# Two mixers issued in the order of the text: ScalarE and VectorE under a hand-written order, with the norm's column moved into the first segment

## The chip, the cores and the metric

The kernel runs on one core of one Trainium2 chip. The metric is the device time of one execution in microseconds; the median over several runs is what two kernels are compared by. The core has five engines that matter here, each with a queue of its own: TensorE (PE in the profile; its weight loads are shown apart, as PEld), VectorE (DVE), ScalarE (ACT), GpSimd (POOL) and SyncE (SP, which issues the loads). An engine issues its instructions in the order in which they stand in its queue, and an instruction waits on semaphores until what it needs is there.

## The reference

A decoder trunk of two layers on one sequence of 256 tokens, 1024 wide, 16 heads of 64, in float32. Each layer is: half a SwiGLU block, a mixer, half a SwiGLU block.

```python
h = x
for layer in range(2):
    h = h + 0.5 * swiglu(rmsnorm(h, ffn1_norm[layer]), gate1, up1, down1)
    hn = rmsnorm(h, mix_norm[layer])
    if layer == 0:
        h = h + mixer_a(hn, ...)     # causal attention, three dilated windows merged
    else:
        h = h + mixer_b(hn, ...)     # causal attention on shared keys and values
    h = h + 0.5 * swiglu(rmsnorm(h, ffn2_norm[layer]), gate2, up2, down2)
    if layer == 0:
        shared = shared_kv(h, kv_norm, kv_w)   # keys and values of layer 1
return rmsnorm(h, final_norm)
```

With 256 tokens the three windows of mixer A become one attention with a mask that holds the logarithm of how often each key counts, and mixer B is plain causal attention. `swiglu(h)` is `(silu(h @ gate) * (h @ up)) @ down`, 2816 wide inside. `rmsnorm` divides each token by the root of its mean square and multiplies by a gain.

## The kernel before

**Numbers in two parts.** Every product is made from high and low parts: a weight piece is loaded raw, ScalarE copies it to the high part (`wh_...`), VectorE subtracts to get the low part (`wl_...`), and TensorE runs high*high, high*low and low*high. So each weight piece costs one ScalarE copy of 128x1024 and one VectorE subtraction of 128x1024 ahead of its products, and activations are treated alike (`parts_of`: a ScalarE copy, and `rest`, a VectorE subtraction). The pieces lie in a ring of eight buffers for `wh` and eight for `wl`; a ninth split waits until TensorE has finished the products of a piece whose buffer comes free.

**The stream** lies transposed in `hT` (part of the tensor `gains_hT`), eight blocks of 128 features by 256 tokens. For each norm, `scale(k)` makes `x_n_k`, block k times its gain in two parts, and `square(k)` makes the square on ScalarE (`sq_n_k`) and adds it into `ss_n` on GpSimd: seven adds, one behind the other, as all go into one tile. `finish()` then multiplies `ss_n` with a column of 1/1024 on TensorE (`col_n`), adds epsilon on VectorE (`v_n`) and raises to -0.5 on GpSimd (`c_n`): the factor of each token. The factor is applied after the products. In the FFN `spread()` also turns it into a row (`diag_n`, `row_n`, `r_n`).

**The mixers.** `mixer` first runs six segments of projections (`projections`), then the output projection (`out_t`). A segment is 16 products: eight blocks of features for two tiles of 128 tokens, in the order features 0 to 3 for tile 0, then tile 1, features 4 to 7 for tile 0, then tile 1. `evacuate` scales a finished tile out of PSUM with the norm's factor; VectorE rotates queries and keys (`rotate`); `turn_in` transposes them on TensorE (`qt`) and splits them (`qkh`, `qkl`); then for each of eight pairs of heads come `scores` (`s`, `sm`, softened by ScalarE, scaled by GpSimd), `turn` (`pt`, split into `pT`) and `values` (`po`, then `o` and `oT`, the blocks of the output projection). In mixer A the first segment needs the norm's factor as soon as it is finished; in mixer B the first segment belongs to another norm, whose factor is known, and the second needs the new one. `out_t` multiplies the eight `oT` blocks with the pieces of `wo` (`wh_ao`, `wl_ao`; `bo` in B) into four accumulators; the last three blocks are held back, and the accumulators finish one after the other; each is added to `hT`, and `scale(d)` follows, and after all eight the eight `square(d)`.

**What sets the order.** The mixers' text is written by an `Agenda`: every step of attention is put on it with a delay, counted in the estimated time of the products, and comes up when the products written so far have passed that time. That gives the order of the text. Behind it, a scheduler goes over the whole program, estimates durations, and lets each engine issue whatever it thinks ready first; the order in an engine's queue is the scheduler's, not the text's. `Pieces` splits weight pieces `LEAD = 4` ahead of their use. The FFN behind a mixer takes its weights by `unit` (`wh_f_g_0`, `wh_f_g_4`, `wh_f_u_0`, `wh_f_u_4`: the two halves of gate and up for two blocks of the inner width). The first such pair of blocks (inner blocks 0 and 1) is multiplied feature by feature, as the `x_n_k` arrive (lines 389 to 404), and then `finish()` writes the column; the pairs 2, 4 and so on follow whole.

Of the kernel before, what the change touches and what calls it, by code (L numbers as in the profile page):

```python
# [29 lines left out]
LEAD = 4  # L30
# [36 lines left out]
def trunk(ctx: ExitStack, tc: tile.TileContext, a: dict, out: bass.AP):  # L67
# [70 lines left out]
    def late_constants():  # L138
        nc.sync.dma_start(rot, a["rot"].rearrange("t p c n -> p t c n"))
        nc.sync.dma_start(masks, a["masks"].rearrange("i p n -> p i n"))  # L140
        nc.sync.dma_start(gfin, a["final_norm"].rearrange("(o d) -> o d", o=1).to_broadcast([P, D]))


    def unit(name, k, n, srcs):

        raw = rawp.tile([P, k, n], F32, tag="raw", name=f"raw_{name}")
        for dst, src in srcs:
            nc.sync.dma_start(raw if dst is None else raw[:, :, dst], src)
        return pieces_of(name, raw, k, n)

    def pieces_of(name, raw, k, n):
        pieces = []
        for j in range(0, k, 1024 // n):
# [4 lines left out]
            nc.scalar.activation(wh, r, AF.Copy)  # L158
            nc.vector.tensor_sub(wl, r, wh.bitcast(F32))  # L159
# [18 lines left out]
    def rows(w, k0, k, c0, n):  # L178
        return w[k0 * P:(k0 + k) * P, c0:c0 + n].rearrange("(k p) n -> p k n", p=P)
# [104 lines left out]
    class Pieces:  # L284
# [29 lines left out]
                    self.rest.pop(0)()  # L314

        def __getitem__(self, i):
            self.split(i + LEAD)
            return self.parts[i]


# [16 lines left out]
        parts_of(hi, lo, flat(q), later=rest.append)  # L337
        return rest

    def ffn_blocks(name, wg, wu, norm, first=None, beside=(), sums=None):  # L340

# [41 lines left out]
        for f in range(0, KF, 2):  # L383
            if f == 0 and first is not None:
                ws = opening(wg, wu, first)
            else:
                ws = zip(*[unit(f"{name}_{n}{f}", KD, S, [(None, rows(w, 0, KD, f * P, S))])
                           for n, w in (("g", wg), ("u", wu))])
            if f == 0:
                acs = [[(trt if i and n == "u" else acc)(f"{name}_{n}{i}") for n in "gu"] for i in range(2)]  # L390
                for k, pair in enumerate(ws):
                    for i in range(2):
                        for ac, (wh, wl) in zip(acs[i], pair):
                            cols = slice(i * P, (i + 1) * P)
                            products_t([ac], [[(wh[:, cols], wl[:, cols])]], norm.x[k:k + 1], k == 0, k == KD - 1)
                    while norm.late:
                        norm.late.pop(0)()
                if first is not None:
                    for k in range(KD - 2, KD):
                        norm.square(k)  # L400
                if norm.col is None:
                    norm.finish()
                done += [(i, *acs[i]) for i in range(2)]
                continue
            pair = list(zip(*ws))
            for call in beside[f // 2 - 1:f // 2]:
                call()
            for i in (f, f + 1):
                acs = both(i, pair)
                close_all()  # L410
                done.append((i, *acs))
# [14 lines left out]
                                for j in range(2))  # L426
        return sums

    def ffn(name, layer, which, norm, after, first=None, beside=(), homes=("kx4", "kx6", "qkh", "qkh")):
        wg, wu, wd = (a[f"ffn{which}_w_{n}"][layer] for n in ("gate", "up", "down"))  # L430
        sums = left_sums(homes)
        blocks = ffn_blocks(name, wg, wu, norm, first, beside, sums)
        if which == 1:
            table(AF.Exp, blocks[-1][:, 0, 0:1].bitcast(F32))
        down(f"{name}_d", wd, blocks, sums, after)
# [141 lines left out]
                part(t, slice(512 + S, 1024), True)  # L577
            after(t)

    def out_t(name, pieces, base, blocks, norm, tail=3):  # L580

        accs = [acc(f"ot_{name}_{i}") for i in range(KD // 2)]

# [8 lines left out]
                nc.tensor.matmul(ac, wl[:, d], hi, start=False, stop=k == KD - 1 and j == 1)  # L592

        for k in range(KD - tail):
            ws = pieces[base + k][0]
            while len(blocks) <= k:
                yield None
            for i in range(KD // 2):
                step(i, k, ws)
                yield 0.72  # L600
# [26 lines left out]
    def attention(agenda, operands, mask, name, blocks):  # L627
# [38 lines left out]
        def turn(p, i):  # L666
            tr = trt(f"pt_{name}{p}_{i}")[:, :3 * P]
            for n in range(3):
                nc.tensor.transpose(tr[:, n * P:(n + 1) * P], sms[p, i][:, n * P:(n + 1) * P], ident)
            pT = pTs[p, i] = pp.tile([P, 2, 3 * P], F32R, tag="pT", name=f"pT_{name}{p}_{i}")  # L670
            parts_of(pT[:, 0], pT[:, 1], tr, later=agenda.soon)

        def values(p):
            g, b = divmod(p, HG // 2)
# [26 lines left out]

        return scores, turn, values

    def mixer(name, segs, plan, wo, mask, after):

# [17 lines left out]
        for norm in {id(norm): norm for norm, _, _ in segs}.values():  # L723
            for i in range(len(norm.late)):
                agenda.after(1.5 + 0.5 * i, lambda norm=norm: norm.late.pop(0)())
        scores, turn, values = attention(agenda, lambda g: (qks[g], vss.get(g)), mask, name, blocks)

        def turns(p):
# [18 lines left out]
        def evacuate(i, t, r, ac, parts):  # L747
# [40 lines left out]

    def first(k, n):
# [21 lines left out]
    def ending(at):  # L811
# [28 lines left out]
    blocks = ffn_blocks("f21", a["ffn2_w_gate"][1], a["ffn2_w_up"][1], n6, beside=[lambda: None] + turns, sums=sums)  # L840

    parts = [[], []]
    outs = [[None, None] for t in range(NT)]
# [63 lines left out]
```

## Time and profile before

| | |
|---|---|
| median of 3 runs | 984.71 us (984.63 to 985.41) |
| the profiled execution | 984.39 us, of which 982.6 us from the first to the last instruction |
| TensorE busy | 968.3 us, 99% of the span |
| VectorE, ScalarE, GpSimd busy | 813.0, 613.8, 289.6 us |
| granted TensorE clock | 0.999 |
| first product of mixer A, first product of the FFN behind it | 190.45 us, 310.02 us |
| first product of mixer B, first product of the FFN behind it | 674.84 us, 793.62 us |

Times are microseconds from the start of the span unless marked ns. A row of the timeline has the start, the duration, the engine, the line, the operation, what it writes and reads (buffer numbers left out), how many instructions are merged into the row, and in brackets how long the engine was idle before it and what released it. Rows of one engine overlap by a little, since an instruction starts while the one before drains. The ends of matmuls are modelled, so their starts are read: from one start to the next.

### The profile page before, as it was taken

The numbers are of one execution on the slowest core, as the hardware profiler recorded it, in microseconds if no ns is written. First come the engines' busy times: TensorE is split into PE (matmuls) and PEld (weight loads), VectorE is DVE, ScalarE is ACT, GpSimd is POOL, SyncE is SP. The second block draws the span as 40 slices with busy tenths as digits, with TensorE's granted clock in tenths as the row PEclk, the third lists the DMA queues.
The fourth block names the chain that finished last, engine by engine and source line by source line (L and its number), as shares of the span: only waits on it lengthen the run. The fifth ranks groups of instructions, "written<-read, shape, count | busy, mean of one in ns | idle before, by whom it ended". The sixth has DMA issues, their size and how long they took to land.

```text
span 982.6 us, 14865 instructions
## 1 busy us (share of the span) xinstructions
PE 968.3 (99%) x5391; PEld 832.8 (85%) x5391; DVE 813.0 (83%) x1383; ACT 613.8 (62%) x1131; POOL 289.6 (29%) x242
## 2 busy tenths in 40 slices
PE   8999999999999999999999999999999999999997
PEld 6888888878889888888888888888788998888886
DVE  7988899887878788889898888987678778888995
ACT  7656657567776566556576655656577766666561
POOL 3211246132342211146032121612142422112461
PEclk9999999999999999999999999999999999999999
DMA  9876636664443565545755555483744345565351
GB/s 317 256 238 186 197 132 217 223 203 155 132 129 106 179 201 178 185 158 210 256 168 176 172 182 205 171 283 109 248 131 129 101 158 170 177 204 180 129 171 43
DMA packets 126857, 176.00 MB, mean 179 GB/s; under 512 B 3392, under 2 KB 106304, under 8 KB 126784
## 3 DMA queue, kind: packets, MB, share of 16 engines
q1 hardware_dynamic: 125936, 174.01, 54.4%
q10 hardware_dynamic: 848, 1.05, 0.3%
q8 instruction: 42, 0.69, 0.3%
q14 instruction: 31, 0.25, 0.1%
HBM read 173.99 MB, written 1.05 MB: 178 GB/s over the span
## 4 chain that ended last, share of the span: by engine, by line
PE 68%; ACT 2%; DVE 2%; issue 1%; POOL 0%; POOLq 0%; ACTq 0%; DVEq 0%
PE f_g L195 12%; PE f_u L195 12%; PE f_u L198 6%; PE f_g L198 6%; PE dn_f_d L188 5%; PE dn_f_d L186 5%; PE dn_f_d L184 5%; PE dn_f_d_m L188 1%; PE dn_f_d_m L186 1%; PE dn_f_d_m L184 1%; PE q_b L184 1%; PE q_b L188 1%; PE q_b L186 1%; PE ot_ao L592 1%; PE ot_ao L590 1%; PE kv_b L184 1%
## 5 line engine op out<-in xcount | busy, mean ns | idle before, releaser
L357 POOL TENSOR_TENSOR j_f_u<-j_f_u,r_n 128x256 f32<-128x256 f32 x88 | 92.3, 1051 | 360.9 <-DVE j_f_u L325 338.1
L195 PE MATMUL f_g<-x_n,wh_f_g 128*128 128x512 f32 x688 | 180.5, 394 | 0.0
L195 PE MATMUL f_u<-x_n,wh_f_u 128*128 128x512 f32 x688 | 177.2, 390 | 0.0
L195 PEld LDWEIGHTS f_u<-x_n,wh_f_u 128*128 128x128 f32 x688 | 129.2, 188 | 27.3
L195 PEld LDWEIGHTS f_g<-x_n,wh_f_g 128*128 128x128 f32 x688 | 124.0, 189 | 22.7
L159 DVE TENSOR_TENSOR wl_f_u<-raw_f_u,wh_f_u 128x1024 fp32r<-128x1024 f32 x86 | 113.1, 1317 | 2.7 <-ACT wh_f_u L158 2.7
L159 DVE TENSOR_TENSOR wl_f_g<-raw_f_g,wh_f_g 128x1024 fp32r<-128x1024 f32 x86 | 104.1, 1229 | 3.9 <-ACT wh_f_g L158 3.9
L198 PE MATMUL f_u<-x_n,wl_f_u 128*128 128x256 f32 x688 | 103.3, 283 | 0.0
L198 PE MATMUL f_g<-x_n,wl_f_g 128*128 128x256 f32 x688 | 102.7, 282 | 0.0
L198 PEld LDWEIGHTS f_g<-x_n,wl_f_g 128*128 128x128 f32 x688 | 96.4, 190 | 6.3
L158 ACT ACTIVATE wh_f_u<-raw_f_u 128x1024 fp32r<-128x1024 f32 x86 | 87.9, 1048 | 13.4 <-PE f_g L195 7.5
L158 ACT ACTIVATE wh_f_g<-raw_f_g 128x1024 fp32r<-128x1024 f32 x86 | 89.5, 1048 | 5.0 <-PE f_g L195 2.8
L198 PEld LDWEIGHTS f_u<-x_n,wl_f_u 128*128 128x128 f32 x688 | 91.6, 192 | 0.0
L355 ACT ACTIVATE j_f_g<-j_f_g 128x256 f32<-128x256 f32 x88 | 36.7, 417 | 87.2 <-DVE j_f_g L354 86.9
L233 POOL TENSOR_TENSOR ss_n<-ss_n,sq_n 128x256 f32<-128x256 f32 x42 | 38.4, 914 | 148.3 <-ACT sq_n L232 146.3
L98 ACT ACTIVATE act_f<-j_f_g 128x256 fp32r<-128x256 f32 x58 | 23.9, 418 | 56.6 <-DVE j_f_g L365 56.6
L365 DVE TENSOR_TENSOR j_f_g<-j_f_g,j_f_u 128x256 f32<-128x256 f32 x58 | 27.9, 487 | 30.1 <-POOL j_f_u L357 30.1
L473 POOL TENSOR_TENSOR sum_f_d_6b<-sum_f_d_6ac,raw_f_d 128x512 f32<-128x512 f32 x4 | 45.5, 11374 | 17.6 <-DVE sum_f_d_6ac L472 13.2
L325 DVE TENSOR_TENSOR j_f_g<-f_g,j_f_g 128x256 f32<-128x256 f32 x88 | 36.7, 417 | 11.9 <-ACT j_f_g L324 11.9
L664 POOL TENSOR_SCALAR sm_b<-sm_b,ls_b 128x128 f32<-128x128 f32 (+1 forms) x32 | 29.8, 949 | 44.0 <-DVE ls_b L662 34.3
L664 POOL TENSOR_SCALAR sm_a<-sm_a,ls_a 128x128 f32<-128x128 f32 (+1 forms) x32 | 28.0, 890 | 50.0 <-DVE ls_a L662 32.8
L324 ACT ACTIVATE j_f_u<-f_u 128x256 f32<-128x256 f32 x88 | 33.0, 375 | 14.7 <-PE row_n L250 13.7
(565 smaller groups left out, 2386.5 us busy)
## 6 DMA issues: line engine op xcount, KB each, us to landing
raw_f_d<-in_ffn_w_down_dram SPq DMA_DIRECT2D x44, 1024.0 KB, 5.0
raw_f_g<-in_ffn_w_gate_dram SPq DMA_DIRECT2D x43, 1024.0 KB, 5.4
raw_f_u<-in_ffn_w_up_dram SPq DMA_DIRECT2D x43, 1024.0 KB, 5.4
raw_qka<-in_a_w_qkv_dram SPq DMA_DIRECT2D x16, 512.0 KB, 4.9
raw_va<-in_a_w_qkv_dram SPq DMA_DIRECT2D x4, 1024.0 KB, 6.0
raw_ao<-in_a_w_o_dram SPq DMA_DIRECT2D x4, 1024.0 KB, 4.9
raw_kvb<-in_kv_w_dram SPq DMA_DIRECT2D x8, 512.0 KB, 4.4
raw_qb<-in_b_w_q_dram SPq DMA_DIRECT2D x4, 1024.0 KB, 5.5
```

Source lines behind the costliest of these rows:

```text
L158: nc.scalar.activation(wh, r, AF.Copy)
L159: nc.vector.tensor_sub(wl, r, wh.bitcast(F32))
L184: nc.tensor.matmul(ac, xh, wh, start=first, stop=False)
L186: nc.tensor.matmul(ac, xh, wl, start=False, stop=False)
L188: nc.tensor.matmul(ac, xl, wh, start=False, stop=last)
L195: nc.tensor.matmul(ac, wh, flat(x), start=first and i == 0, stop=False)
L198: nc.tensor.matmul(ac[:, :S], wl, x[:, 0, :], start=False, stop=last and i == len(ws) - 1)
L233: nc.gpsimd.tensor_tensor(self.ss, self.ss, sq, op=ALU.add)
L325: nc.vector.tensor_add(s, ac[:, :S], s)
L357: nc.gpsimd.tensor_tensor(u, u, norm.row, op=ALU.mult)
L473: nc.gpsimd.tensor_tensor(b[:, 0], ac[:, 0], raw[:, 3], op=ALU.add)
L664: nc.gpsimd.tensor_scalar(sm[:, seg], sm[:, seg], ls[:, t:t + 1], None, op0=ALU.mult)
```

## The change

`mixer` now runs both of its stages inside `tc.manual_schedule` for ScalarE and VectorE: what is written there is issued by these two engines in the order of the text. TensorE, GpSimd and SyncE stay with the scheduler. Four things go with it.

- The norm's column: if it is not known when the mixer begins, `finish()` is put on the agenda 8.1 after the start, so it comes up within the first segment, after 12 of its 16 products. Each token tile is now evacuated when its own products are done, where before both waited for the end of the segment. In the first segment the transposes of tile 0 and tile 1 are put on the agenda apart (4.4 and 3.2 after their evacuation).
- `turn` remembers the two instructions that split `pT` of pair p (`marks[p]`), and `queued(p)` puts what is written inside it behind them, on the engines of these two.
- In `out_t` of mixer A the pieces that are split at blocks 3 and 4 are queued behind the `pT` of pairs 4 and 5. Mixer B passes none.
- The first four splits of the FFN behind each mixer are queued behind `pT` of pairs 5, 6, 7, 7 (A) and 4, 5, 6, 7 (B).

In the queues of the changed program SyncE and GpSimd have the same instructions in the same order as before. On TensorE `col_n` and `qt` of the first segments, some `po`, and the beginning of the FFN behind each mixer stand elsewhere. ScalarE and VectorE differ through both mixers and the first blocks behind them.

```diff
+    marks = {}
+
+    def queued(p):
+        stack = ExitStack()
+        for ins in marks.get(p, ()):
+            stack.enter_context(tc.issue_after(ins.ins))
+        return stack
...
-    def unit(name, k, n, srcs):
+    def unit(name, k, n, srcs, behind=()):
...
-            nc.scalar.activation(wh, r, AF.Copy)
-            nc.vector.tensor_sub(wl, r, wh.bitcast(F32))
+            with queued(next(behind, None)):
+                nc.scalar.activation(wh, r, AF.Copy)
+                nc.vector.tensor_sub(wl, r, wh.bitcast(F32))
...
         for k in range(KD - tail):
-            ws = pieces[base + k][0]
+            with queued(queue.get(k)):
+                ws = pieces.get(base + k)[0]
...
-            parts_of(pT[:, 0], pT[:, 1], tr, later=agenda.soon)
+            hi = nc.scalar.activation(pT[:, 0], tr, AF.Copy)
+
+            def rest():
+                marks[p] = [hi, nc.vector.tensor_sub(pT[:, 1], tr, pT[:, 0].bitcast(F32))]
+
+            agenda.soon(rest)
...
+            if norm.col is None:
+                agenda.after(8.1, norm.finish)
...
-                    agenda.after(3.2, turn_in, g, t)
+                    agenda.after(4.4 - 1.2 * t if i == 0 else 3.2, turn_in, g, t)
...
-                        if k0 + 4 == KD and norm.col is not None:
+                        if k0 + 4 == KD:
                             evacuate(i, t, norm.col[t], acs[t], parts)
-                if norm.col is None:
-                    norm.finish()
-                    for t in range(NT):
-                        evacuate(i, t, norm.col[t], acs[t], parts)
-
-        agenda.run(projections())
-        agenda.run(out_t(f"{name}o", pieces, base, blocks, after))
+
+        with tc.manual_schedule(engines={mybir.EngineType.Activation, mybir.EngineType.DVE}):
+            agenda.run(projections())
+            agenda.run(out_t(f"{name}o", pieces, base, blocks, after, queue))
...
-          a["a_w_o"][0], masks[:, 0, :], n2)
-    ffn("f20", 0, 2, n2, n3)
+          a["a_w_o"][0], masks[:, 0, :], n2, {3: 4, 4: 5})
+    ffn("f20", 0, 2, n2, n3, queue=(5, 6, 7, 7))
...
+                        queue=(4, 5, 6, 7))
```

More of the change, by code (lines that the diff above doesn't have):

```diff
@@ L148, in unit @@
             nc.sync.dma_start(raw if dst is None else raw[:, :, dst], src)
-        return pieces_of(name, raw, k, n)
-    def pieces_of(name, raw, k, n):
         pieces = []
+        behind = iter(behind)
         for j in range(0, k, 1024 // n):
@@ L316, in __getitem__, with get @@
         def __getitem__(self, i):
-            self.split(i + LEAD)
+            return self.get(i)
+        def get(self, i, lead=LEAD):
+            self.split(i + lead)
             return self.parts[i]
@@ L338, in quarter_sums, with ffn_blocks @@
         return rest
-    def ffn_blocks(name, wg, wu, norm, first=None, beside=(), sums=None):
+    def ffn_blocks(name, wg, wu, norm, first=None, beside=(), sums=None, queue=()):
         blocks, pairs, rest = [], {}, []
@@ L386, in ffn_blocks @@
             else:
-                ws = zip(*[unit(f"{name}_{n}{f}", KD, S, [(None, rows(w, 0, KD, f * P, S))])
-                           for n, w in (("g", wg), ("u", wu))])
+                ws = zip(*[unit(f"{name}_{n}{f}", KD, S, [(None, rows(w, 0, KD, f * P, S))], behind[:2 if f == 0 else 0])
+                           for n, w, behind in (("g", wg, queue[:2]), ("u", wu, queue[2:]))])
             if f == 0:
@@ L427, in left_sums, with ffn @@
         return sums
-    def ffn(name, layer, which, norm, after, first=None, beside=(), homes=("kx4", "kx6", "qkh", "qkh")):
+    def ffn(name, layer, which, norm, after, first=None, beside=(), homes=("kx4", "kx6", "qkh", "qkh"), queue=()):
         wg, wu, wd = (a[f"ffn{which}_w_{n}"][layer] for n in ("gate", "up", "down"))
         sums = left_sums(homes)
-        blocks = ffn_blocks(name, wg, wu, norm, first, beside, sums)
+        blocks = ffn_blocks(name, wg, wu, norm, first, beside, sums, queue)
         if which == 1:
@@ L578, in down_last, with out_t @@
             after(t)
-    def out_t(name, pieces, base, blocks, norm, tail=3):
+    def out_t(name, pieces, base, blocks, norm, queue, tail=3):
         accs = [acc(f"ot_{name}_{i}") for i in range(KD // 2)]
@@ L702, in attention, with mixer @@
         return scores, turn, values
-    def mixer(name, segs, plan, wo, mask, after):
+    def mixer(name, segs, plan, wo, mask, after, queue={}):
         n = HG * DH
@@ L839, in trunk @@
     turns = [lambda t=t, c=c: turn_h(t, c) for t in range(NT) for c in range(2)]
-    blocks = ffn_blocks("f21", a["ffn2_w_gate"][1], a["ffn2_w_up"][1], n6, beside=[lambda: None] + turns, sums=sums)
+    blocks = ffn_blocks("f21", a["ffn2_w_gate"][1], a["ffn2_w_up"][1], n6, beside=[lambda: None] + turns, sums=sums,
+                        queue=(4, 5, 6, 7))
     parts = [[], []]
```

## The prediction

> **What bounds the kernel now.** I read the page's head first, then the waits of TensorE, then the timeline around each wait, and last the windows and rows at the beginning of the FFN behind each mixer. The head:
>
> ```profile
> span 982.6 us, 14865 instructions
> PE 968.3 (99%) x5391; PEld 832.8 (85%) x5391; DVE 813.0 (83%) x1383; ACT 613.8 (62%) x1131; POOL 289.6 (29%) x242
> ```
>
> TensorE is in use 99% of the span, so nothing that the other engines save is worth anything by itself. The change can only win what TensorE waits inside the mixers, and it loses whatever it makes TensorE wait. These are TensorE's waits in the mixers (engine, line, released by, us in total, times, longest):
>
> ```profile
> PE qt_a L741 <- DVE rt_a L625: 1.7, 1, 1.7
> PE qt_b L741 <- DVE rt_b L625: 1.0, 1, 1.0
> PE po_b L683 <- DVE pT_b L94: 1.0, 1, 1.0
> PE po_a L683 <- DVE vs_a L96: 0.8, 1, 0.8
> PE po_a L683 <- DVE pT_a L94: 0.7, 1, 0.7
> ```
>
> Together 5.2 us: half a per cent is the most that a better order can bring.
>
> **Mixer A, first segment.** The column and what hangs on it, in the timeline:
>
> ```profile
> 195.78 4.45 POOL L233 TENSOR_TENSOR ss_n<-ss_n,sq_n 128x256 f32<-128x256 f32 x4 [3.86 <-ACT sq_n L232]
> 201.23 3.48 DVE L312 TENSOR_TENSOR wl_qka<-raw_qka,wh_qka 128x1024 fp32r<-128x1024 f32 x3
> 202.07 0.39 PE L184 MATMUL qk_a<-wh_qka,x_n 128*128 128x512 f32 x1
> 202.76 0.50 PE L238 MATMUL col_n<-mean,ss_n 128*128 128x1 f32 x4
> 204.64 0.15 DVE L240 TENSOR_SCALAR v_n<-col_n 128x2 f32<-128x2 f32 x1
> 204.87 1.62 POOL L242 TENSOR_TENSOR c_n<-v_n,expo 128x2 f32<-128x2 f32 x1 [4.64 <-DVE v_n L240]
> 206.53 1.27 ACT L752 ACTIVATE rt_a<-qk_a,c_n 128x512 f32<-128x512 f32 x2 [2.51 <-POOL c_n L242]
> 208.46 1.23 PE L741 MATMUL qt_a<-ident,rt_a 128*128 128x128 f32 x8 [1.65 <-DVE rt_a L625]
> ```
>
> `col_n` is multiplied at 202.76, but `v_n` comes at 204.64, since three subtractions of `wl_qka` stand ahead of it on VectorE. Then c_n, rt_a, the rotation, and `qt` waits 1.65. Three matmuls of a product take 202.76 - 202.07 = 0.69 us. After the change the column stands four products earlier: 202.76 - 4 x 0.69 = 200.0. The four adds end at 195.78 + 4.45 = 200.23, so it may wait 0.2 there (between 0 and 0.7, one product). `v_n` no longer stands behind the three subtractions, which takes away most of the 1.9 us from 202.76 to 204.64; with the 2.8 of the four products the chain comes over 4 us earlier, and `qt` (now two lots of four, one per token tile, behind later products) finds its input. What is next in line there is the lateness of the adds themselves. Gain 1.65, plus some 0.45 that the `x_n` blocks and the column's own place cost today, less 0.2: I take -1.9, bounds -1.0 (a wait at the column of one product, 0.7) and -2.4.
>
> **Mixer B, first segments.** The same move; here the new norm's column was late by the 1.0 of `qt_b`. -0.95, bounds 0 and -1.1: the first segment of B uses the old norm, so the column has a whole segment more and only the order of `v_n` and `rt_b` counts.
>
> **The segments between.** The same instructions, VectorE and ScalarE in the text's order. By the changed queues and the durations of before, each `pT`, `s` and `qk` is ready when TensorE comes to it, at the tightest by some 0.2. I take 0, because the waits above have no other row of a mixer over 0.7; bounds -0.5 and +3 (one subtraction of 1.23 in front of a `pT` or a rotation at two or three places).
>
> **The output projections.** A piece split ahead of time costs one copy and one subtraction of 128x1024, `pT`'s low half costs half a microsecond:
>
> ```profile
> 282.40 1.05 ACT L310 ACTIVATE wh_ao<-raw_ao 128x1024 fp32r<-128x1024 f32 x1
> 287.03 0.54 DVE L94 TENSOR_TENSOR pT_a<-pt_a,pT_a 128x384 fp32r<-128x384 f32 x1
> 793.35 1.23 DVE L159 TENSOR_TENSOR wl_f_g<-raw_f_g,wh_f_g 128x1024 fp32r<-128x1024 f32 x1 [0.29 <-ACT wh_f_g L158]
> ```
>
> In A the two waits at `po_a`, 0.8 + 0.7, go: the splits that stood in front of `vs_a` and `pT_a` are queued behind `pT`. But with the order fixed, VectorE now has `wl_ao_3_1` in front of the last pairs' `o_a6` and `pT`, and two FFN subtractions (`wl_f_u_0`, `wl_f_u_4`) in front of the low half of `oT_a7`. Each is 1.23, most of which lies beside products; I count 0.35 and 0.6 as showing. Net -0.5, bounds -1.5 (nothing shows) and +1.0 (two whole subtractions show, 2.46 - 1.5). In B no output pieces are queued: `wl_bo_3_1` waits for its copy, which stands behind the high half of `pT_b6`, and itself stands in front of that pair's low half. The old wait of 1.0 goes, a new one of up to 1.05 + 1.23 less the cover of the products comes: 0, bounds -1.0 and +1.3.
>
> **The beginning of the FFN behind each mixer: here is the loss.** These are rows of before, mixer B first, then the same places behind mixer A, then the adds as a group (mean ns: least/median/most):
>
> ```profile
> 789.82 0.41 DVE L609 TENSOR_TENSOR gains_hT<-ot_bo,gains_hT 128x256 f32<-128x256 f32 x1
> 790.00 0.40 ACT L232 ACTIVATE sq_n<-gains_hT 128x256 f32<-128x256 f32 x1
> 790.16 0.47 DVE L96 SCALAR_TENSOR_TENSOR x_n<-gains_hT,x_n 128x256 fp32r<-128x256 f32 x1
> 790.31 0.50 ACT L98 ACTIVATE x_n<-gains_hT 128x256 fp32r<-128x256 f32 x1
> 792.26 1.06 ACT L158 ACTIVATE wh_f_g<-raw_f_g 128x1024 fp32r<-128x1024 f32 x1 [0.44 <-PE ot_bo L591]
> 793.62 0.40 PE L195 MATMUL f_g<-x_n,wh_f_g 128*128 128x512 f32 x1
> 799.00 2.01 ACT L158 ACTIVATE wh_f_g<-raw_f_g 128x1024 fp32r<-128x1024 f32 x2 [0.96 <-PE f_g L195]
> 804.93 0.50 PE L238 MATMUL col_n<-mean,ss_n 128*128 128x1 f32 x4
> ```
> ```profile
> 310.02 0.40 PE L195 MATMUL f_g<-x_n,wh_f_g 128*128 128x512 f32 x1
> 312.97 1.63 POOL L233 TENSOR_TENSOR ss_n<-ss_n,sq_n 128x256 f32<-128x256 f32 x2 [1.13 <-ACT sq_n L232]
> 321.33 0.50 PE L238 MATMUL col_n<-mean,ss_n 128*128 128x1 f32 x4
> 321.69 2.09 PE L195 MATMUL f_g<-x_n,wh_f_g 128*128 128x512 f32 x8
> 321.87 0.16 DVE L240 TENSOR_SCALAR v_n<-col_n 128x2 f32<-128x2 f32 x1 [2.45 <-PE col_n L238]
> ```
> ```profile
> 310.02:321.33 11.31, 11.31 (x66) 9.82 (x65) 9.40 (x11) 7.02 (x12) 3.09 (x4) 1.00 0.56 175
> L233 POOL TENSOR_TENSOR ss_n<-ss_n,sq_n x42: 737/805/1805, 8.9 to 798.7; 128x256 f32<-128x256 f32 x42
> ```
>
> Today ScalarE squares the blocks between the scalings (790.00 stands among the `x_n`), and the last adds behind mixer A run at 312.97 to 314.60: 6.7 us before `col_n` at 321.33. In the window from the first FFN product to the column TensorE has 11.31 us of work and no gap. Behind the change the text decides, and the text writes the eight squares after all eight scalings. ScalarE's queue there reads: x_n 0 to 4, `wh_f_g4_0`, x_n 5, `wh_f_g4_4`, x_n 6, x_n 7, and only then the eight squares. (g4 is the gate of the third pair of inner blocks, 4 and 5; 0 and 4 are its two halves.) `wh_f_g4_0` is a ninth split: it needs the buffer that TensorE reads until block 3 of the first pair. So everything behind it, squares included, waits for TensorE. With F as the first FFN product (793.62):
>
> - `wh_f_g4_0` begins at F+5.4 (799.00, there too with a wait for f_g) and ends, 1.06 later, at F+6.4. VectorE is held likewise: `wl_f_g4_0`, 1.23, to F+7.7, the low half of x_n 5, 0.47, to F+8.1, the residual's add of the next block, 0.41, to F+8.5, `wl_f_g4_4` to F+9.7, x_n 6 to F+10.1, the last add to F+10.5.
> - x_n 7's copy, 0.50, to F+11.0; then the first two squares, 0.40 each, partly begun as soon as the last block is there: F+11.5.
> - GpSimd's seven adds, one behind the other, at 0.74 to 0.81 each (the group's least and median): 5.2 to 5.6. The sum is ready at F+16.7 to F+17.1, and TensorE sees it some 0.1 later.
> - TensorE in its new order has, ahead of `col_n`, the first pair's products and 11 high products of the next pair: 11.31 + 11 x 0.24 (eight take 2.09 in the row above, whose last 0.39 is a whole matmul: (2.09 - 0.39) / 7) = F+13.9.
>
> TensorE stands at the column for 2.9 to 3.3 us; I take 3.2. It is in order, so 21 products and `row_n` queue behind it. VectorE stands at `v_n`, with `wl_f_u4_0`, `diag_n` and `wl_f_u4_4` behind it; ScalarE's four evacuations of the first pair wait for the factor. These are late by the same 3 us and so is TensorE; I count no second wait for them, 0 to +0.7 each. SyncE's and GpSimd's queues keep their order, so loads are not moved; GpSimd only starts later. Bounds for one start: 0 (the column ready in time) and 4.5 (adds at 1.0 as in the 4.45 row of four, since some do run beside VectorE's work). Twice: +6.4, bounds 0 and +9.
>
> A page of the Trainium skill, GPSIMD Engine Reference, section 1 (Specifications, the row on SBUF interfaces), says that GpSimd shares its interfaces with VectorE and contends with VectorE instructions of two SBUF inputs. That would put the adds at their least, as VectorE is parked at `v_n`; the trace's spread from 737 to 1805 ns agrees in direction. By it alone each start would lose 0.4 less than at the median, within what is taken above.
>
> **The sum.** -1.9 - 0.95 + 0 - 0.5 + 0 + 6.4 = +3.05. The profiled execution took 984.39 (its span 982.6 and 1.8 around it), 0.3 below the median of 984.71. So 987.4 for a profiled execution and 987.8 for the median. About 0.2%, 2.0 us, is what a measurement tells from no change.
>
> **The rivals.** R1, the column's sum is ready in time and only the gains stay: 984.7 - 3.35 = 981.4, faster. It decides at one point: the last add must end by F+13.9, so the adds must begin by F+8.5, 3 us earlier than I have it; that happens if the buffer that `wh_f_g4_0` waits for is free already when block 4 is scaled, about F+2.5. Against it: 799.00, the same wait in today's order. For it: my times rest on an order read from the queues, with durations of another order.
>
> R2, the wait is half of what I have (adds at 0.74, squares begun earlier, TensorE later by small waits at x_n 5 to 7): 1.6 twice, so 984.7 - 3.35 + 3.2 = 984.6, no change that can be measured.
>
> R3, the fixed order also puts waits where I have none, in the segments and output projections (a subtraction of 1.23 in front of a short instruction at two or three places): +3, 990.8. For it: VectorE is 83% busy, and a blocked head of its queue blocks all; against it: TensorE's later products need what VectorE made several microseconds before.
>
> R4, the wait at the column lets TensorE's clock fall. The kernel's first matmuls, and a window with a wait:
>
> ```profile
> 5.49 0.63 PE L195 MATMUL f_u<-x_n,wh 128*128 128x512 f32 x1
> 5.92 0.63 PE L195 MATMUL f_g<-x_n,wh 128*128 128x512 f32 x1
> 7.53 0.46 PE L195 MATMUL f_g<-x_n,wh 128*128 128x512 f32 x1
> 7.82 0.40 PE L195 MATMUL f_u<-x_n,wh 128*128 128x512 f32 x1
> 186.95:213.95 27.00, 25.35 (x128) 19.90 (x127) 24.09 (x35) 18.29 (x30) 8.48 (x8) 1.00 0.48 157
> ```
>
> The first products are 0.43 apart, from 7.53 on 0.29 and less: after idleness TensorE runs for 2 us or more at little over half its rate. The wait of 1.65 in mixer A did not do this (granted 1.00). If 3.2 does, each start loses another 0.9 or more (2.0 us from 5.49 to 7.53 at 0.24 / 0.43 of the rate; those before 5.49 are slow too, so I take 1.3): 987.8 + 2.6 = 990.4. The Trainium skill, TensorE: Matmul & The Clock Gate, part 1, What's actually happening, has the rule: an idle window of about 3.4 us, free-running, halves the clock, and about as long of work brings it back. By that page each such fall costs 1.7, so 991.2; a wait of 3.2 is just short of its window. No run here yet shows a wait of this length in the middle of the kernel.
>
> **How the numbers follow.** My forecast 0.53; R1 0.12; R2 0.17; R3 0.12; R4 0.06. The likeliest gives 987.8. R1 is faster, and a sliver of R2: 0.14 faster; 0.17 the same; 0.69 slower. The range from 983.0 to 991.0 leaves out R1 and the far ends of R3 and R4. The likeliest case's own range is 986.4 to 989.5, from 2.9 to 3.3 at each column and the nearer bounds of the mixers' terms.
>
> **What the changed profile would show.** Right: two waits of TensorE at `col_n` (L238 of before) behind GpSimd's adds, some 3 us each, the seven adds back to back after the last `x_n`; no wait at `qt_a` and `qt_b`; waits at `po` of under 1 in A. Wrong: `col_n` without a wait (R1); a wait there but TensorE late already at x_n 5 to 7 (R2); new waits at `po`, `s`, `pt` or in the segments (R3); a granted clock below 1.00 just behind the column (R4). What would turn it over is the squares: if they run before `wh_f_g4_0`, the loss is gone and the kernel is faster.

## The result, and the profile after

The changed kernel takes 991.39 us (median of 6 runs, 987.88 to 991.95) against 984.62 for the kernel before beside it: ratio 1.0062, 95% interval 1.0048 to 1.0077. It is slower, as forecast, but by 6.8 us where 3.1 were forecast; the median lies 0.4 us above the upper end of the predicted range. The profiled execution took 990.43 (span 988.6).

The head of the page, and then TensorE's waits, all that are not at the kernel's very beginning (engine, line, released by, us in total, times, longest):

```profile
span 988.6 us, 14824 instructions
PE 972.5 (98%) x5391; PEld 836.4 (85%) x5391; DVE 806.4 (82%) x1383; ACT 615.0 (62%) x1131; POOL 288.4 (29%) x242
```
```profile
PE col_n L246 <- POOL ss_n L241: 5.9, 2, 2.9
...
PE po_a L701 <- DVE o_a L710: 0.4, 1, 0.4
PE po_b L701 <- DVE o_b L710: 0.3, 1, 0.3
PE ot_ao L603 <- DVE oT_a L94: 0.2, 1, 0.2
```

The waits at `qt` and the waits of 1.0, 0.8 and 0.7 at `po` are gone, and 0.9 came in their place. Two waits of 2.9 us at `col_n` are new. TensorE also shows 4.2 us more of busy time for the same 5391 matmuls: some of them ran slower.

Where the time went is seen from the start times of a few matmuls (us from the span's start):

| first matmul of | before | after | after - before |
|---|---|---|---|
| mixer A | 190.45 | 190.30 | -0.15 |
| its output projection | 278.80 | 276.17 | -2.63 |
| the FFN behind it | 310.02 | 306.65 | -3.37 |
| `row_n` in that FFN | 327.36 | 330.34 | +2.97 |
| mixer B | 674.84 | 678.04 | +3.21 |
| its output projection | 760.86 | 763.06 | +2.20 |
| the FFN behind it | 793.62 | 794.63 | +1.01 |
| `row_n` in that FFN | 810.96 | 816.99 | +6.03 |

So the mixers gained 3.2 and 2.2 us, 5.4 together, and the beginnings of the two FFNs lost 6.3 and 5.0. Everything else kept its length to within 0.3 us.

The timeline of the FFN's beginning behind mixer A, ordered by engine (ScalarE, GpSimd, TensorE, VectorE):

```profile
312.05 1.06 ACT L166 ACTIVATE wh_f_g<-raw_f_g 128x1024 fp32r<-128x1024 f32 x1 [1.31 <-PE f_g L203]
...
317.00 0.51 ACT L98 ACTIVATE x_n<-gains_hT 128x256 fp32r<-128x256 f32 x1 [1.35 <-DVE gains_hT L622]
317.41 0.40 ACT L237 ACTIVATE ss_n<-gains_hT 128x256 f32<-128x256 f32 x1
317.72 2.50 ACT L240 ACTIVATE sq_n<-gains_hT 128x256 f32<-128x256 f32 x7
...
318.20 5.59 POOL L241 TENSOR_TENSOR ss_n<-ss_n,sq_n 128x256 f32<-128x256 f32 x7 [35.96 <-ACT sq_n L240]
...
306.65 0.40 PE L203 MATMUL f_g<-x_n,wh_f_g 128*128 128x512 f32 x1
...
323.85 0.94 PE L246 MATMUL col_n<-mean,ss_n 128*128 128x1 f32 x4 [2.94 <-POOL ss_n L241]
...
324.82 0.16 DVE L248 TENSOR_SCALAR v_n<-col_n 128x2 f32<-128x2 f32 x1 [6.80 <-PE col_n L246]
```

With F = 306.65: the ninth split begins at F+5.4, the last scaling at F+10.4, the squares at F+10.8, the seven adds run back to back from F+11.6, and the column is multiplied at F+17.2. VectorE stood at `v_n` for 6.8 us.

And the matmuls from the column to the next pair of blocks, as windows (stretch, its length, busy us and count for PE, PEld, DVE, ACT, POOL, then the granted clock, DMA share, GB/s), first A, then B:

```profile
323.85:330.92 7.07, 7.07 (x29) 6.59 (x30) 3.58 (x7) 0.36 (x1) 1.64 (x1) 0.52 0.20 54
811.81:817.35 5.54, 5.54 (x29) 5.06 (x30) 3.59 (x7) 0.36 (x1) 1.65 (x1) 0.69 0.01 2
```

Twenty-nine matmuls need 7.07 x 0.52 = 3.7 us at the full clock, and 5.54 x 0.69 = 3.8; they took 3.4 and 1.7 more. The clock had fallen to half when TensorE began again. TensorE stood for 2.9 us by the list of waits, which counts from the modelled end of the last matmul; it was 3.1 counted from where the next product could have started, 0.24 after the last one's start. So 3.1 us of waiting and 3.4 of half rate are mixer A's 6.3 to within 0.2, and 3.1 and 1.7 are B's 5.0 to within 0.2. In the kernel before, the products behind the column ran at 1.00:

```profile
321.33:327.72 6.39, 6.39 (x42) 5.72 (x41) 3.90 (x8) 2.67 (x5) 0.72 (x1) 1.00 0.59 186
```

From run to run the changed kernel's mean granted clock goes from 0.991 (991.95 us) to 0.998 (987.88 us), so its spread of 4 us goes largely with the clock.

### The profile page after: what moved, and what is told of

It reads as the page before. It is cut to its first block, busy times and chain, and to the rows that moved or that the text cites. A ratio compares the mean times of both kernels' runs of the same rounds, so it can differ in the third digit from the quotient of the medians.

```text
span 988.6 us, 14824 instructions
## 1 busy us (share of the span) xinstructions
PE 972.5 (98%) x5391; PEld 836.4 (85%) x5391; DVE 806.4 (82%) x1383; ACT 615.0 (62%) x1131; POOL 288.4 (29%) x242
## 4 chain that ended last, share of the span: by engine, by line
PE 92%; DVE 3%; ACT 2%; issue 1%; POOL 1%; DMA 0%; SPq 0%; POOLq 0%; DVEq 0%; ACTq 0%
PE f_u L203 16%; PE f_g L203 15%; PE f_g L206 8%; PE f_u L206 8%; PE dn_f_d L194 6%; PE dn_f_d L192 6%; PE dn_f_d L196 6%; PE qk_a L192 2%; PE qk_a L196 1%; PE qk_a L194 1%; PE dn_f_d_m L194 1%; PE dn_f_d_m L192 1%; PE dn_f_d_m L196 1%; POOL ss_n L241 1%; PE v_a L192 1%
## 5 line engine op out<-in xcount | busy, mean ns | idle before, releaser
L368 POOL TENSOR_TENSOR j_f_u<-j_f_u,r_n 128x256 f32<-128x256 f32 x88 | 88.5, 1008 | 359.4 <-DVE j_f_u L336 339.4
L203 PE MATMUL f_u<-x_n,wh_f_u 128*128 128x512 f32 x688 | 179.7, 393 | 0.0
L241 POOL TENSOR_TENSOR ss_n<-ss_n,sq_n 128x256 f32<-128x256 f32 x42 | 35.3, 840 | 172.5 <-ACT sq_n L240 170.2
L98 ACT ACTIVATE x_n<-gains_hT 128x256 fp32r<-128x256 f32 x48 | 23.7, 500 | 40.1 <-DVE gains_hT L555 28.0
L677 POOL TENSOR_SCALAR sm_b<-sm_b,ls_b 128x128 f32<-128x128 f32 (+1 forms) x32 | 31.8, 1011 | 53.4 <-DVE ls_b L675 53.3
L677 POOL TENSOR_SCALAR sm_a<-sm_a,ls_a 128x128 f32<-128x128 f32 (+1 forms) x32 | 32.0, 1014 | 48.3 <-DVE ls_a L675 46.3
```

The source lines that it names most:

```text
L98: nc.scalar.activation(hi, src, AF.Copy, scale=scale)
L203: nc.tensor.matmul(ac, wh, flat(x), start=first and i == 0, stop=False)
L241: nc.gpsimd.tensor_tensor(self.ss, self.ss, sq, op=ALU.add)
L368: nc.gpsimd.tensor_tensor(u, u, norm.row, op=ALU.mult)
L677: nc.gpsimd.tensor_scalar(sm[:, seg], sm[:, seg], ls[:, t:t + 1], None, op0=ALU.mult)
```

## The experiments

The theory that these profiles suggest: (1) the fixed order in the mixers gains 5.4 us; (2) in the output projection it makes the squares, and so the norm's column, late; (3) the wait at the column lets the clock fall, which costs as much again. The rivals are that it is the ninth split alone that holds the squares, that the column's new place makes the gain and not the order, and that the slow matmuls have another cause than the wait.

### Squares and splits at the FFN's beginning

**The squares right behind the scalings** (`sq_between`):

```diff
                 norm.scale(d)
-        for d in range(KD):
-            norm.square(d)
+                norm.square(d)
```

> The changed kernel, with each square written right behind the scaling of its block, no longer after all eight. Theory (the squares' place in ScalarE's fixed order makes the column late): no wait at the column over 0.5, clock 1.00, and the mixers' gain of 5.4 us (3.2 to the FFN behind mixer A, 2.2 behind B) stays: about 979.5, between 978.5 and 981. Rival (the fixed order of the FFN's beginning as a whole is the loss, splits and scalings too): 983 or more, with new waits at the FFN's first products.

Measured: 982.44 us, ratio 0.9980 (0.9971 to 0.9989), clock 0.998 to 0.999. The wait at the column and the fall of the clock are both gone, so the squares' place is what made the column late. But 979.5 was not reached; the theory's number missed by 3, and the time lies between the two expectations. TensorE's waits now:

```profile
PE f_g L203 <- DVE x_n L96: 1.3, 4, 0.5
PE f_g L206 <- DVE wl L182: 0.9, 1, 0.9
PE f_g L203 <- DVE gains_hT L622: 0.6, 2, 0.3
```

(The middle one is at the kernel's beginning and not new.) The first FFN's products wait for `x_n` and for the residual's adds. From the first FFN product to `row_n` it is 19.1 us (306.87 to 326.00) where it was 17.3: a loss of some 1.8 us in A, and as much in B, that the column had covered. The listed waits, counted from modelled ends, show only half of it.

**The ninth split behind the squares** (`f4_behind`):

```diff
-... rows(w, 0, KD, f * P, S))], behind[:2 if f == 0 else 0])
+... rows(w, 0, KD, f * P, S))], behind[:2] if f == 0 else ["sq"] * 2 if f == 4 and n == "g" and queue else ())
...
         for d in range(KD):
-            norm.square(d)
+            marks["sq"] = [norm.square(d)]
```

> The changed kernel with its squares where they are, but the two gate splits of the third pair of inner blocks, the first of which waits for a free buffer, queued behind the last square. Theory (what holds the squares is the ninth split's wait for TensorE, not that they stand after all scalings): scalings and squares run through, the column is ready when TensorE comes to it (wait under 0.5), 979 to 981. Rival (standing after all eight scalings is enough to be late): a wait of 1.5 to 3 at each column stays, 983 to 989.

Measured: 989.98 us (985.76 to 991.69), ratio 1.0045 (1.0031 to 1.0060). The theory falls; the rival's wait is there, and the time lies 1 us above the rival's range. TensorE's wait, and the timeline of ScalarE, GpSimd and TensorE:

```profile
PE col_n L247 <- POOL ss_n L241: 5.9, 2, 3.0
```
```profile
313.86 0.51 ACT L98 ACTIVATE x_n<-gains_hT 128x256 fp32r<-128x256 f32 x1 [0.89 <-DVE gains_hT L623]
315.26 0.51 ACT L98 ACTIVATE x_n<-gains_hT 128x256 fp32r<-128x256 f32 x1 [0.89 <-DVE gains_hT L623]
315.67 0.40 ACT L237 ACTIVATE ss_n<-gains_hT 128x256 f32<-128x256 f32 x1
...
316.46 5.59 POOL L241 TENSOR_TENSOR ss_n<-ss_n,sq_n 128x256 f32<-128x256 f32 x7 [33.86 <-ACT sq_n L240]
322.11 1.01 PE L247 MATMUL col_n<-mean,ss_n 128*128 128x1 f32 x4 [2.86 <-POOL ss_n L241]
```

With the first FFN product at 307.01 the column comes at F+15.1 instead of F+17.2: the ninth split's wait is worth 2.1 us of lateness. TensorE, however, now has fewer products ahead of the column (it stops at F+12.2, where it stopped at F+14.3) and waits as long as before. And without the split in the way each scaling still waits 0.89 for the residual's add of its block: ScalarE's copy, VectorE's low half and VectorE's add of the next block follow each other at 1.40 us per block (313.86 to 315.26), so the eighth scaling is at F+8.3 at best, and the squares behind it.

**Both** (`sq_f4`): the two edits above together.

> The run sq_between, with the two gate splits of the third pair of inner blocks queued behind the last square as in f4_behind. Theory (what is left of the loss in sq_between, 1.8 us at each FFN start, is x_n 5 to 7 held behind the ninth split): the waits at x_n go and the time is about 979. Rival (the scalings are late by VectorE's fixed order, where each block's add and low half alternate with a subtraction of 1.2 us): 981.5 to 982.5 as in sq_between.

Measured: 980.99 us, ratio 0.9966 (0.9952 to 0.9980); between the two expectations. `x_n` is still waited for, 0.5 instead of 1.3, and `gains_hT` 0.6 as before. The ninth split was worth 1.5 of the 3.6 us that `sq_between` had left. The rest, 2.1, is put down to the alternation of the scalings with VectorE's adds because of the waits that are left; no run takes the alternation away by itself.

### Which half of the mixer

**The fixed order in the projections alone** (`proj_only`):

```diff
         with tc.manual_schedule(engines={...}):
             agenda.run(projections())
-            agenda.run(out_t(f"{name}o", pieces, base, blocks, after, queue))
+        agenda.run(out_t(f"{name}o", pieces, base, blocks, after, queue))
```

> The changed kernel with the fixed order for the projections alone; the output projection and what stands in it are again the scheduler's. Theory: the column has no wait, the gain up to the first output product stays (2.5 in A, 1.0 in B), the gain from there to the FFN (0.7 in A, 1.2 in B) goes: 984.7 - 3.5 = 981.2. Rival (the fixed order in the projections gains only together with the output projection's): 983 to 985.

Measured: 977.96 us, ratio 0.9934 (0.9920 to 0.9949), clock 0.998 to 0.999: 3 us better than expected, and better than both kernels. The gain up to the FFN is 3.75 in A and 2.64 in B, more than in the changed kernel itself (3.2 and 2.2), and nothing is given back. The gain between the first output product and the FFN, which the theory gave up, is there too: 1.3 in A and 1.9 in B. All that is left of TensorE's waits in the mixers, and the window from the first FFN product to the column:

```profile
PE po_a L701 <- DVE vs_a L96: 0.2, 1, 0.2
```
```profile
306.27:317.58 11.31, 11.31 (x66) 9.80 (x65) 9.40 (x11) 6.92 (x12) 3.77 (x4) 1.00 0.55 174
```

The window is the 11.31 of before. The scheduler puts the scalings in twos, the squares behind them, and the next pair's splits last; the last adds end 6.7 us before the column:

```profile
307.50 0.89 ACT L98 ACTIVATE x_n<-gains_hT 128x256 fp32r<-128x256 f32 x2
308.29 0.71 ACT L240 ACTIVATE sq_n<-gains_hT 128x256 f32<-128x256 f32 x2
...
308.84 2.06 POOL L241 TENSOR_TENSOR ss_n<-ss_n,sq_n 128x256 f32<-128x256 f32 x2 [0.50 <-ACT sq_n L240]
```

**The fixed order in the output projections alone** (`out_only`):

```diff
-        with tc.manual_schedule(engines={...}):
-            agenda.run(projections())
+        agenda.run(projections())
+        with tc.manual_schedule(engines={...}):
             agenda.run(out_t(f"{name}o", pieces, base, blocks, after, queue))
```

> The changed kernel with the fixed order for the output projections alone; the projections are the scheduler's. Theory (the loss is the output projection's fixed order and needs nothing of the projections'): the gains of early_only (1.5) and of the output projections (0.7 and 1.2), then the two columns and the clock as in the changed kernel (6.3 and 5.0 in its profile): 984.4 - 3.4 + 11.3 = 992, between 988 and 994, with the granted clock under 0.997. Rival (the loss comes only where both are fixed): 981 to 984.

Measured: 991.57 us, ratio 1.0066 (1.0050 to 1.0081), clock 0.994 to 0.997; as the theory said. The waits at the columns are those of the changed kernel (the third is one of 0.6 ahead of mixer B):

```profile
PE col_n L246 <- POOL ss_n L241: 6.4, 3, 2.9
```

Together the two runs say that the whole loss comes from the fixed order in the output projection. They do not say that the whole gain comes from the other half: from the first product of a mixer to that of its FFN this run still gains 1.7 us in A and 1.6 in B, with the scheduler's order in the projections.

**No fixed order, but the column early and the tiles one by one** (`early_only`, made from the kernel before):

```diff
+            if norm.col is None:
+                agenda.after(8.1, norm.finish)
...
-                    agenda.after(3.2, turn_in, g, t)
+                    agenda.after(4.4 - 1.2 * t if i == 0 else 3.2, turn_in, g, t)
...
-                        if k0 + 4 == KD and norm.col is not None:
+                        if k0 + 4 == KD:
                             evacuate(i, t, norm.col[t], acs[t], parts)
-                if norm.col is None:
-                    norm.finish()
-                    for t in range(NT):
-                        evacuate(i, t, norm.col[t], acs[t], parts)
```

> The kernel before, with the column put on the agenda within the first segment and the token tiles evacuated and transposed one by one, but no fixed order: the scheduler keeps ScalarE and VectorE. Theory (the first segments' gain is the column's place): the two waits at the first transposes go, 984.4 - 2.7 = 981.7. Rival (without the fixed order the scheduler leaves the column's addition behind subtractions, as it did): 983.5 to 984.7.

Measured: 983.17 us (982.77 to 984.90), ratio 0.9989 (0.9980 to 0.9999). Between the two: 1.4 of the 2.7. What is left of the waits at `qt` is 0.2 at a time, but a wait of 0.6 at `col_n` comes in, and those at `po` stay.

**The fixed order in the projections, but the column late** (`late_fixed`, made from `proj_only` by taking the edit above back).

> The kernel of the run proj_only (fixed order in the projections alone), but with the column at the end of the first segment and both tiles evacuated there, as before. Theory (column and order each have a part): the waits at the first transposes, 2.7 together, come back, and the rest of the 6.4 us stays: 980.6. Rivals: all of the gain is the column's, 984; all of it is the fixed order's, 978.

Measured: 979.11 us, ratio 0.9946 (0.9931 to 0.9961). It lies between the expectations, nearer to the fixed order's. The waits at `qt` do not come back although the column stands where it stood before:

```profile
PE qt_a L759 <- DVE rt_a L638: 0.2, 1, 0.2
PE qt_b L759 <- DVE rt_b L638: 0.2, 1, 0.2
```

With the fixed order `v_n` comes at 202.68, 0.5 us behind `col_n` (202.14), where three subtractions had put 1.9 between them. So the order on VectorE alone is enough to take the waits at `qt` away. The column's place alone takes them away too (`early_only`), with one subtraction still ahead of `v_n`. Up to A's output projection the order alone gains 1.8 us, the place alone 0.8, both together 2.5. Beside the order, the column's place is worth 1.2 us of the whole time.

**Nothing queued behind `pT`** (`proj_noqueue`): `proj_only` without its three `queue` arguments.

> The run proj_only without any split queued behind a pT (neither the output pieces of mixer A nor the first splits of the FFNs). Theory (in the output projection, where proj_only gained 1.3 in A and 1.9 in B although the scheduler sets the order there, the gain is from the splits being queued): 978 + 3.1 = 981. Rival (the queueing changes nothing that shows): 978.

Measured: 980.21 us, ratio 0.9952 (0.9935 to 0.9968), 2.2 us more than `proj_only`. A `po_b` wait is back that the queueing had removed:

```profile
PE po_b L701 <- DVE pT_b L687: 1.0, 1, 1.0
```

The queueing is worth 1.9 us in B's output projection and 0.2 in A's. The runs also take the gain of `proj_only` apart, which the two halves alone did not: the column's place and the single tiles bring 1.4 us (`early_only` against the kernel before), the fixed order in the projections some 3.0 (`proj_noqueue`, 980.21, against `early_only`, 983.17), and the queueing 2.2.

### Is it the wait that slows the clock?

Matmuls of no use are written just ahead of the column of the two norms, so that TensorE works where it waited. The first form (`filler`) used the squares as operands:

```diff
             ps = trt(f"col_{self.name}")
+            if self.name in ("n2", "n6"):
+                for sq in self.sqs[:4] * 2:
+                    nc.tensor.matmul(ps[:, :S], ident, sq, start=True, stop=True)
```

> The changed kernel, with 8 matmuls of no use (identity times four of the squares) written just ahead of the column of the two norms that follow a mixer, so that TensorE works where it waited. They compute nothing that is used. Theory (the column's sum is late, and the wait also lets the clock fall): the sum is ready as late as before (first FFN product + 17.2), the wait shrinks to under 1.5, the granted clock stays at 1.00, the half-rate stretches of about 6.6 and 3.5 us behind the columns are gone, and the time is 990.4 less about 5.1, so 985 to 986, with little spread from run to run. Rival (the clock is not what slows the products behind the column, or it falls whatever TensorE does): 990 to 992 as in the changed kernel.

Measured: 998.05 us (995.98 to 998.75), ratio 1.0134 (1.0119 to 1.0149), clock 0.992 to 0.995. It decides nothing: the last squares and adds came later, so that the column stood at F+19.7 and no longer at F+17.2 (most likely because the matmuls held the squares' buffers, which no run shows apart), and the wait at the column was 2.9 us again, with a fall of the clock behind it.

The second form reads `x_n_7` only (`filler2`, 14 of them; `filler3`, 22):

```diff
+                for i in range(14):
+                    nc.tensor.matmul(ps, self.x[7][:, 0, :P], flat(self.x[7]), start=True, stop=True)
```

> The changed kernel with 14 matmuls of 128x512 of no use just ahead of the column of the two norms that follow a mixer, on x_n_7 alone, so that the buffers of the squares are not touched; they are some 3.2 us of work and compute nothing that is used. Theory (a wait of about 3 us lets the clock fall): the sum comes 17.2 behind the first FFN product as before, the wait shrinks to about 1.0, the granted clock stays at 1.00 behind the column, and the time is some 987.5 with little spread: 984.4, less 5.4 of gains in the mixers, and at each column 4.3 (the column at 17.2 instead of 11.3, with 25 products still to do behind it instead of 32). Rival (the clock falls whatever TensorE does there): 990 to 993.

> The run filler2 with 22 matmuls of no use in place of 14: 1.8 us more work for TensorE at each of the two columns, in a place where it waited 2.4 us with 14. Theory (a wait of 2.4 us is still long enough for the clock to fall, one of 0.6 isn't): the column comes at the same moment as in filler2, the wait is about 0.6, the clock stays at 1.00, and what filler2 lost behind its columns in the profiled execution (3.3 us in A, 1.8 in B against the same products at the full rate) is not lost: 995.5 - 5.0 = 990.5, faster with more work. Rival (the clock does not hang on the wait): 995 to 996, or more by the added work.

Measured: `filler2` 995.54 us (991.92 to 995.96), ratio 1.0105 (1.0087 to 1.0123), clock 0.993 to 0.999; `filler3` 991.42 us (991.26 to 991.49), ratio 1.0064 (1.0049 to 1.0079), clock 0.998 to 0.999. In `filler2` the column came at F+19.0, since its adds were slower than expected (see the last section), so that a wait of 2.4 us was left, and the clock fell; its number missed by 8. In `filler3` the wait is 0.6, the clock stays, and the kernel is 4 us faster with 1.8 us more of work at each column. The row of the column behind mixer A and the window from it to the next pair of blocks, `filler2` and then `filler3`:

```profile
325.68 1.01 PE L249 MATMUL col_n<-mean,ss_n 128*128 128x1 f32 x4 [2.42 <-POOL ss_n L241]
```
```profile
325.68:333.67 7.99, 7.99 (x33) 7.12 (x34) 1.64 (x6) 0.37 (x1) 0.72 (x1) 0.58 0.37 127
```
```profile
325.79 0.61 PE L249 MATMUL col_n<-mean,ss_n 128*128 128x1 f32 x4 [0.63 <-POOL ss_n L241]
```
```profile
325.79:330.68 4.89, 4.89 (x33) 4.50 (x34) 1.64 (x6) 0.36 (x1) 0.72 (x1) 1.00 0.60 203
```

The column comes at the same moment (325.7 and 325.8), and the same products behind it take 8.0 us at a clock of 0.58, or 4.9 at 1.00. The waiting makes the clock fall: ScalarE, VectorE and GpSimd have the same instructions in the same order in both, and only TensorE's work ahead of the column differs. It does not fall every time. One of the four runs of `filler2` has a mean clock of 0.999 and takes 991.92, close to `filler3`.

## Why the prediction was right, and where it was not

- **What bounds the kernel**: right that only TensorE's waits count, but 5.2 us was called the most that a better order can bring, and `proj_only` brings 6.4. The list of waits counts from modelled ends of matmuls, so its sum is no upper bound.
- **Mixer A, first segment**: -1.9 forecast for the start. The gain up to the output projection was 2.5 (-2.63 against -0.15). Of the two reasons given, the three subtractions ahead of `v_n` are the larger (1.8 alone, `late_fixed`) and the column's place the smaller (0.8 alone, `early_only`). Mis-sized by 0.6, which includes the segments between, taken as 0; the runs do not part the two.
- **Mixer B, first segments**: -0.95 forecast, -1.0 measured.
- **The output projections**: A -0.5 forecast, -0.7 measured. B 0 forecast, -1.2 measured: the wait at `po_b` went and only 0.3 came in its place. I charged B with the split of `wl_bo_3_1` in front of a `pT` and left out what queueing the FFN's splits saves; with the scheduler's order in the output projection it is 1.9 us in B (`proj_noqueue`).
- **The FFN's beginning**: the main step, and right in its place, cause and size up to the column. F+17.2 against F+16.7 to F+17.1 forecast; a wait of 3.1 against 3.2, counted as the forecast counted it. The bullet on the ninth split was half right: the split held the squares by 2.1 us (`f4_behind`), but they stand behind eight scalings that go one block per 1.40 us with VectorE, and with the split out of the way TensorE still waited 2.9 to 3.0 us at the column. "What would turn it over is the squares" was right in direction: `sq_between` is faster than before, though by 2.0 us only, not 5.4, for the scalings are late too.
- **The adds**: at the least duration (0.72 to 0.75 us each), as the prediction's sentence from the Trainium skill (GPSIMD Engine Reference, section 1, Specifications) had it, but at a cadence of 0.81 from start to start (5.59 for seven).
- **The step that failed is the clock.** The sum has no term for it: after the wait the products were taken to run at the full rate. "The wait at the column lets TensorE's clock fall" stood only as the rival R4, with 0.06, and it is what happened, in both places. It cost 3.4 and 1.7 us in the profiled execution, where R4 had 1.3 each.
- The sum worked out again with the measured terms is -5.4 of gains, +6.2 of waits and +5.1 of half rate, +5.9 in all; the profile's difference is 990.43 - 984.39 = 6.0.
- Where the forecast's numbers come near, it is luck. The gains were 2.1 us too small (3.35 against 5.4) and the losses 4.9 too small (6.4 against 11.3), and the two errors offset each other in part. R4's 990.4, 1 us under the measured 991.39, has the same two errors, with losses of 9.0. The fastest run, 987.88, is near the forecast of 987.8 in the same way: with the measured gains and waits it would be 985.2 without any fall of the clock. Its mean clock is 0.998, and what took the other 2.7 us in it is not shown.
- The mistake in R4 was to take a wait of 3.2 as safe because it is "just short" of an idle window of 3.4. By the rule of the Trainium skill (TensorE: Matmul & The Clock Gate, part 1, What's actually happening) a full window of that length must be idle; here waits of 2.4 to 3.0 did it. In `filler2` TensorE was still busy for 1.0 of the 3.4 us ahead of the fall (322.23 to 325.64). The other half of the Trainium skill's rule agrees: the half rate lasted about one such window in B (3.4 us) and two in A (6.8).
- R1, R2 and R3 did not happen: the column did wait, for its full length, and no new wait over 0.4 stood in the segments or output projections.

## What to carry to other kernels

Take an order out of a scheduler's hands only where the text is better than it: here the same construct gained some 3 us in one half of a stage and cost 13 in the other (977.96 without it there, 991.39 with it), and one line of indentation tells them apart. When a norm's sum is fed at the end of a stage, put the squares beside the scalings and the next weights' splits behind both, and count what a fixed queue holds behind an instruction that waits. And when a step of the sum leaves TensorE waiting for 2.4 us or more, as here, price the clock too: the wait can cost its own length a second time.

## What was not expected of the hardware

- The granted clock fell to 0.50 behind waits of 2.4 to 3.0 us, and not behind one of 0.63 (`filler3`) or, in the kernel before, of 1.65; where the limit lies between 1.65 and 2.4 was not measured. In each profiled execution that shows a fall it stayed there for some 3.4 or 6.8 us, and which of the two does not go with the mixer: 6.8 behind A and 3.4 behind B in the changed kernel and in `filler2`, the other way round in `out_only` and `filler`, 6.8 behind both in `f4_behind`. So what such a wait costs is different from run to run: the mean clock of the changed kernel's runs lies between 0.991 and 0.998.
- GpSimd and VectorE slow each other. In `filler2` the scheduler moved two subtractions ahead of `v_n`, so that they ran beside the adds. Two subtractions took 2.97 us in a row, where two alone take 2.4 (1.22 each in the changed kernel), and two of the seven adds took about 1.6 instead of 0.74. The timeline's row, and the adds as a group (least, median and most, in ns):

```profile
321.28 2.97 DVE L167 TENSOR_TENSOR wl_f_u<-raw_f_u,wh_f_u 128x1024 fp32r<-128x1024 f32 x2 [3.17 <-ACT wh_f_u L166]
```
```profile
L241 POOL TENSOR_TENSOR ss_n<-ss_n,sq_n x7: 722/740/1602, 318.3 to 324.9; 128x256 f32<-128x256 f32 x7
```

The Trainium skill tells of contention between GpSimd and VectorE instructions of two SBUF inputs (GPSIMD Engine Reference, section 1, Specifications). The trace agrees; here its price is some 0.86 us on each of the two adds. The power for the column shows it as well: 1.62 us in mixer A before, beside a subtraction, and 0.71 after, when VectorE stood still:

```profile
201.27 0.71 POOL L250 TENSOR_TENSOR c_n<-v_n,expo 128x2 f32<-128x2 f32 x1 [2.37 <-DVE v_n L248]
```
